# Gate and up projections by seven half-size products in a float32 encoder layer

## The chip, the core and the metric

The kernel runs on one core of a Trainium2 chip. The metric is the time of one execution on the device in microseconds; the number used is the median over runs. TensorE (PE in the profile) does matrix products, VectorE (DVE), ScalarE (ACT) and GpSimd (POOL) elementwise work, and SyncE (SP) issues the DMA transfers here. Products accumulate in PSUM banks of 128 partitions by 512 float32; everything else is staged in SBUF.

## The reference

One encoder layer and a last norm, for two sequences with the same weights: `x_prompt` of 512 tokens and `x_sample` of 1024, each of width 1024. Cut to what matters here:

```
x = x + hybrid_mixer(rmsnorm(x, norm1_g), w_in, ..., w_out)      # attention and linear attention
hn = rmsnorm(x, norm2_g)
x = x + (silu(hn @ w_gate) * (hn @ w_up)) @ w_down               # 1024 -> 2816 -> 1024
y = rmsnorm(x, final_norm_g)
```

All is float32. The 1536 tokens of both sequences go through the feed-forward part together, since it treats each token alone.

## The kernel before

A float32 product is made of three passes. Each operand is split into a high part `h` and a rest `l` (`split`, L66 to L69: the cast that makes `h` runs on ACT, L68, the subtraction that makes `l` on DVE, L69), and a product sums h·h, h·l and l·h in PSUM (`mm3`, L82 to L84, and in the same way L982).

The mixer comes first (up to L867): projections, attention, linear attention. Its end is the output projection of the second sequence (`Out`, tile `acco`, products at L82 to L84, added to the residual at L760). In between the last tiles of it the first six token tiles of the feed-forward part are made ready: `Block.rows` loads a tile of 128 tokens (`hx`, three buffers), squares and sums it on ACT (L898), scales it on DVE (L900); `Block.turn` transposes it on PE into a PSUM tile `trf` (L915) and splits that into `hbh` and `hbl`, the transposed input, 8 slices of the model dimension by 768 tokens.

The feed-forward part runs two blocks of 6 token tiles (768 tokens), and in each block 11 groups of 256 of the 2816 feed-forward columns:

- `raw_gu` (L924) loads the group's columns of `w_gate` and `w_up` (`rw_gate`, `rw_up`), `load_gu` splits them by tiles of 128 columns into `hw_gate` and `hw_up` (128 x 1024 elements each, L68 and L69).
- `gate_up` (L982): per tile of 128 columns, weight, slice of the model dimension and pass, two matmuls of 384 tokens into two banks `gu`; 8 slices x 3 passes x 2 halves of the tokens = 48 matmuls a tile and weight, 192 a group. ACT applies silu to gate (L989), DVE multiplies by up (L990) and the result is split into `g`.
- `down` of the group before stands behind the group's gate and up products: the weights `rd` (L999) are split into `wd`, 72 matmuls of 512 columns (L82 to L84) run into banks `dn`, and DVE adds each bank to the residual `xa` (L1018).
- At a block's last group `final` (L1035 to L1050) makes the last norm of each token tile and stores it.

Block 1's input is made ready while block 0 still has two `down` stages to run: the transposes stand between the steps of the last but one (L1059 to L1071), and the gate and up products of block 0's last group, which need the buffers `hbh` and `hbl`, are over by then.

What runs on an engine follows the order of its instruction stream, which a scheduler sets from the program's order; waits are on semaphores. Tiles come from pools with a fixed number of buffers, so a load into a tile waits until the last reader of the buffer that it takes has gone by: `wr` (raw weights) has three buffers, `wh` (split gate and up weights) four, `wd` three, `g` two, `hx` three.

## Time and profile before

| | us |
|---|---|
| median of three runs | 2030.09 (2027.62 to 2030.62) |
| span of the profiled execution | 2028.6 |
| PE busy | 2000.8 |
| DVE busy | 1042.3 |
| ACT busy | 715.2 |
| POOL busy | 80.9 |

The span is the time from the first to the last instruction of one execution under the profiler; it stands 1.5 us under the median of the runs. Busy time of an engine is the time in which an instruction of it was under way. PE's matmuls are pipelined: one that is listed with 0.34 us begins 0.17 us after the one before it, so the rate is read from the starts and not from the durations.

### The profile page before, as it was taken

Reading aid. Unit: us, or ns where it says so; the run is one execution under the profiler, and the core shown is the slowest. Engines: PE = TensorE matmul, PEld = TensorE weight load, DVE = VectorE, ACT = ScalarE, POOL = GpSimd, SP = SyncE. Lnnn points to the kernel's source line nnn. Section 1 sums busy time; section 2 is a strip of 40 time slices with the busy share of each in tenths; the row PEclk is TensorE's granted clock in tenths of the full one; section 3 lists DMA queues with packets and bytes.
Section 4 is the critical chain, followed back from the end, with each engine's and each line's share of the span. In section 5 each row is a group of like instructions: output and inputs, shape, how many; then the busy total and the mean of one; then the engine's idle time right before and its main releaser. Section 6 shows DMA issues by size and latency. Waiting matters only on the chain.

```text
span 2028.6 us, 31825 instructions
## 1 busy us (share of the span) xinstructions
PE 2000.8 (99%) x12740; PEld 1855.8 (91%) x12740; DVE 1042.3 (51%) x2500; ACT 715.2 (35%) x1730; POOL 80.9 (4%) x113
## 2 busy tenths in 40 slices
PE   8999999999999999999999999999999999999997
PEld 7888889899888889999999999999899999999996
DVE  5677766557576776444333333343633343333335
ACT  6665566455454554323111111211432211111112
POOL 1110010111000000000000000000110000000001
PEclk9999999999998999999999999999999999999999
DMA  5232221102220340855211111221341111211101
GB/s 144 61 100 73 65 80 35 51 26 68 68 79 17 105 137 29 284 175 187 63 63 63 63 63 63 63 63 63 114 167 63 63 63 63 63 63 63 63 22 63
DMA packets 149445, 163.13 MB, mean 80 GB/s; under 512 B 15856, under 2 KB 127536, under 8 KB 149296
## 3 DMA queue, kind: packets, MB, share of 16 engines
q1 hardware_dynamic: 149296, 161.09, 25.5%
q8 instruction: 100, 1.64, 0.3%
q14 instruction: 49, 0.40, 0.1%
HBM read 140.02 MB, written 21.04 MB: 79 GB/s over the span
## 4 chain that ended last, share of the span: by engine, by line
PE 92%; DMA 2%; DVE 2%; ACT 2%; issue 1%; POOL 1%; SPq 0%; POOLq 0%; DVEq 0%; ACTq 0%
PE gu L982 36%; PE acc L82 6%; PE acc L84 6%; PE acc L83 6%; PE dn L82 6%; PE dn L83 6%; PE dn L84 6%; PE sc L300 3%; PE pv L400 2%; PE acco L82 2%; PE trp L377 2%; PE acco L83 2%; PE acco L84 2%; PE kv L641 2%; PE trf L915 1%
## 5 line engine op out<-in xcount | busy, mean ns | idle before, releaser
L982 PE MATMUL gu<-hbh,hw_gate 128*128 128x384 f32 x1408 | 310.1, 336 | 0.0
L982 PE MATMUL gu<-hbh,hw_up 128*128 128x384 f32 x1408 | 308.5, 336 | 0.0
L982 PEld LDWEIGHTS gu<-hbh,hw_gate 128*128 128x128 f32 x1408 | 250.1, 188 | 1.8 <-ACT hbh L68 0.3
L982 PEld LDWEIGHTS gu<-hbh,hw_up 128*128 128x128 f32 x1408 | 249.9, 188 | 0.0
L1018 DVE TENSOR_TENSOR xa<-dn,xa 128x512 f32<-128x512 f32 x264 | 177.9, 689 | 113.7 <-PE dn L84 113.6
L83 PE MATMUL dn<-wd,g 128*128 128x512 f32 x528 | 205.5, 389 | 0.0
L84 PE MATMUL dn<-wd,g 128*128 128x512 f32 x528 | 205.4, 389 | 0.0
L82 PE MATMUL dn<-wd,g 128*128 128x512 f32 x528 | 205.3, 390 | 0.0
L982 PE MATMUL gu<-hbl,hw_gate 128*128 128x384 f32 x704 | 180.1, 336 | 0.0
L982 PE MATMUL gu<-hbl,hw_up 128*128 128x384 f32 x704 | 179.3, 336 | 0.0
L68 ACT CAST wd<-rd 128x1024 fp32r<-128x1024 f32 x44 | 45.9, 1049 | 378.0 <-PE dn L84 262.8
L990 DVE TENSOR_TENSOR e<-e,gu 128x384 f32<-128x384 f32 x88 | 44.8, 551 | 246.1 <-PE gu L982 246.1
L68 ACT CAST hw_up<-rw_up 128x1024 fp32r<-128x1024 f32 x44 | 46.2, 1049 | 278.4 <-PE gu L982 278.4
L69 DVE TENSOR_TENSOR hw_gate<-rw_gate,hw_gate 128x1024 fp32r<-128x1024 f32 x44 | 53.9, 1225 | 167.2 <-ACT hw_gate L68 167.2
L982 PEld LDWEIGHTS gu<-hbl,hw_gate 128*128 128x128 f32 x704 | 127.3, 188 | 0.0
L982 PEld LDWEIGHTS gu<-hbl,hw_up 128*128 128x128 f32 x704 | 127.2, 188 | 0.0
L84 PEld LDWEIGHTS dn<-wd,g 128*128 128x128 f32 x528 | 99.1, 188 | 20.7
L82 PEld LDWEIGHTS dn<-wd,g 128*128 128x128 f32 x528 | 99.1, 188 | 20.5 <-DVE xa L1018 0.7
L83 PEld LDWEIGHTS dn<-wd,g 128*128 128x128 f32 x528 | 99.2, 188 | 19.8 <-DVE wd L69 0.2
L69 DVE TENSOR_TENSOR wd<-rd,wd 128x1024 fp32r<-128x1024 f32 x44 | 54.1, 1236 | 108.7 <-ACT wd L68 108.7
L356 ACT ACTIVATE sm<-sm,st 128x256 f32<-128x256 f32 (+1 forms) x160 | 86.7, 543 | 58.4 <-DVE st L350 58.2
L989 ACT ACTIVATE e<-gu 128x384 f32<-128x384 f32 x88 | 38.5, 489 | 161.9 <-PE gu L982 161.9
(320 smaller groups left out, 4142.2 us busy)
## 6 DMA issues: line engine op xcount, KB each, us to landing
rw_gate<-w_gate SPq DMA_DIRECT2D x22, 1024.0 KB, 5.3
rw_up<-w_up SPq DMA_DIRECT2D x22, 1024.0 KB, 5.3
rd<-w_down SPq DMA_DIRECT2D x22, 1024.0 KB, 5.0
wr_ata<-w_in SPq DMA_DIRECT2D x32, 192.0 KB, 2.6
wr_atb<-w_in SPq DMA_DIRECT2D x32, 192.0 KB, 2.6
wt<-lsed SPq DMA_DIRECT2D x32, 128.0 KB, 3.2
mr_b<-mixd_b SPq DMA_DIRECT2D x8, 512.0 KB, 5.7
xr_b<-x_sample SPq DMA_DIRECT2D x8, 512.0 KB, 4.7
```

Source lines behind the costliest of these rows:

```text
L68: nc.scalar.copy(out=h, in_=src)
L69: nc.vector.tensor_tensor(out=l, in0=src, in1=h.bitcast(F32), op=ALU.subtract)
L82: nc.tensor.matmul(out, xh, wh, start=(k == 0), stop=False)
L83: nc.tensor.matmul(out, xh, wl, start=False, stop=False)
L84: nc.tensor.matmul(out, xl, wh, start=False, stop=(k == n - 1))
L300: nc.tensor.matmul(outs[hd], lhs(x[b:b + 64]), rhs(y[b:b + 64]), start=(n == 0), stop=(n == 2))
L356: nc.scalar.activation(out=sm[:, cs], in_=sm[:, cs], func=AF.Exp, scale=0.125, bias=st[:, NM, pat, hd, i0 + g:i0 + g + 1], accum_out=st[:, ...
L377: nc.tensor.transpose(tr[:, i], sm[:, i * P:(i + 1) * P], ident)
L400: nc.tensor.matmul(self.pv[b:b + 64, i * P:(i + 1) * P], v, ptt[hd][:, n], start=(first and n == 0), stop=(last and n == 3),)
L982: nc.tensor.matmul(ps[wi, hf], wt[:, part, k], src[:, k, hf * H:(hf + 1) * H], start=(k == 0 and part == 0 and src is hb), stop=(k == KD - ...
L990: nc.vector.tensor_tensor(out=e, in0=e, in1=ps[1, hf], op=ALU.mult)
L1018: nc.vector.tensor_tensor(out=acc[i][:, cs], in0=ps, in1=acc[i][:, cs], op=ALU.add)
```

## The change

Gate and up are no longer multiplied out directly. For a weight, a group and a block the product (256 columns of the weight, over 1024 of the model dimension, by 768 tokens) is cut into halves along all three: two tiles of 128 columns, two halves of the model dimension (KH = 4 slices each), and two halves of the tokens (even and odd token tiles, H = 384). The eight half-size products are replaced by seven of sums and differences of halves (the variant with shared partial sums):

- Inputs: seven matrices `b11, t2, b21, t3, t1, t4, b22`, each in a high and a low part, in place of `hbh` and `hbl`. `Block.turn(q)` makes them for a pair of token tiles: 16 transposes, one copy, four subtractions, seven splits. Three turns make a block, where there were six of two splits each.
- Weights: `Weights.prepare(n)` makes the operand of product n: `s1`, `s2` and two sums made in place in the raw tile (four DVE operations a weight, line L1004 of the new kernel) and seven splits of 128 x 512 (`cw_gate...`, `cw_up...`) in place of two splits of 128 x 1024.
- Products: `Group.product` runs 12 matmuls of 128 x 384 (4 slices x 3 passes) into one bank `gu`; products 2, 5 and 6 go on accumulating in the banks of 0, 3 and 4. Two weights x 7 x 12 = 168 matmuls a group in place of 192.
- Evictions: `common` copies product 0 (ACT, L1050 of the new kernel) and adds the others on DVE (L1047) into the partial sums `u2`, `u3` and `c21`, before silu and the multiplication, which are as many as before.
- Order of work: seven products of gate, `down` of the group before, seven products of up. Weights are prepared four products ahead (AHEAD). At the end of a block `down` of the last group stands directly behind its last up product, and the making of block 1's input stands between the steps of that last `down`.
- Buffers: `wr` 3 to 2 (and allocated only when the mixer's buffers are released), `wd` 3 to 2, `g` 2 to 1, `hx` 3 to 2, `wh` replaced by `wc` with six of half the size, `e` 3 to 7, new `sm` with two. The first group's raw weights are no longer loaded two tiles before the end of the output projection. `final` writes into `xa` in place, and its gain `fg` is loaded later.

```diff
         hb_p = pool(right, "hb", 1, side="right")
         cf = pool(right, "cf", 1, side="right")
-        hx_p = pool(right, "hx", 3, side="right")
+        hx_p = pool(right, "hx", 2, side="right")
         tf_p = pool(right, "tf", 3, side="right")
-        wr_p = pool(right, "wr", 3, side="right")
+        sm_p = pool(right, "sm", 2, side="right")
...
-        H = NT * P // 2
+        NP = NT // 2
+        H = NP * P
+        KH = KD // 2
...
-                self.hb = hb_p.tile([P, KD, NT * P], F32R, tag="h", name=f"hbh{blk}")
-                self.lb = hb_p.tile([P, KD, NT * P], F32R, tag="l", name=f"hbl{blk}")
+                self.B = {
+                    x: [hb_p.tile([P, KH, H], F32R, tag=f"{x}{w}", name=f"{x}{w}_{blk}") for w in "hl"]
+                    for x in ("b11", "t2", "b21", "t3", "t1", "t4", "b22")
+                }
                 self.acc, self.hx = {}, {}
...
+            def turn(self, q, tr_p, tag):
+                x = [self.hx.pop(2 * q), self.hx.pop(2 * q + 1)]
+                cs = slice(q * P, (q + 1) * P)
+                def quarter(k, t):
+                    tr = tr_p.tile([P, KH, P], F32, tag=tag, name="trf")
+                    for n in range(KH):
+                        nc.tensor.transpose(tr[:, n], x[t][:, (KH * k + n) * P:(KH * k + n + 1) * P], ident)
+                    return tr
+                def put(nm, src):
+                    h, l = self.B[nm]
+                    split(h[:, :, cs], l[:, :, cs], src)
+                sub = lambda o, i0, i1: nc.vector.tensor_tensor(out=o, in0=i0, in1=i1, op=ALU.subtract)
+                t3, t1 = [sm_p.tile([P, KH, P], F32, tag="sm", name=n) for n in ("xt3", "xt1")]
+                tr = quarter(0, 1)
+                nc.scalar.copy(out=t3, in_=tr)
+                tr = quarter(0, 0)
+                put("b11", tr)
+                sub(t1, t3, tr)
+                tr = quarter(1, 1)
+                put("t1", t1)
+                sub(t1, tr, t1)
+                put("t2", t1)
+                sub(t3, tr, t3)
+                put("b22", tr)
+                tr = quarter(1, 0)
+                put("t3", t3)
+                put("b21", tr)
+                sub(t1, tr, t1)
+                put("t4", t1)
...
-            if j + 2 == sb.T:
-                for wn in ("w_gate", "w_up"):
-                    raw_gu(0, 0, wn)
...
+                blocks[0].rows(1)
+            if 0 <= q < NP:
+                blocks[0].turn(q, tr_p, "tr")
+                if q + 1 < NP:
+                    blocks[0].rows(2 * q + 2)
+                    blocks[0].rows(2 * q + 3)
-        wh_p = pool(left, "wh", 4, side="left")
-        wd_p = pool(left, "wd", 3, side="left")
-        g_p = pool(left, "g", 2, side="left")
-        e_p = pool(left, "e", 3, side="left")
+        wr_p = pool(left, "wr", 2, side="left")
+        wc_p = pool(left, "wc", 6, side="left")
+        wd_p = pool(left, "wd", 2, side="left")
+        g_p = pool(left, "g", 1, side="left")
+        e_p = pool(left, "e", 7, side="left")
...
+        class Weights:
...
+            def prepare(self, n):
+                r = raws[self.key]
+                a11, a12, a21, a22 = [r[:, KH * k:KH * k + KH, P * f:P * f + P] for f in range(2) for k in range(2)]
+                tt = lambda o, i0, i1, op: nc.vector.tensor_tensor(out=o, in0=i0, in1=i1, op=op)
+                if n == 1:
+                    self.s1, self.s2 = [sm_p.tile([P, KH, P], F32, tag="sm", name=f"{x}{self.nm}") for x in ("s1", "s2")]
+                    tt(self.s1, a21, a22, ALU.add)
+                    tt(self.s2, self.s1, a11, ALU.subtract)
+                elif n == 3:
+                    tt(a21, a11, a21, ALU.subtract)
+                elif n == 6:
+                    tt(a12, a12, self.s2, ALU.subtract)
+                src = [a11, None, a12, a21, None, a22, a12][n]
+                src = self.s2 if n == 1 else self.s1 if n == 4 else src
+                wc = wc_p.tile([P, 2, KH, P], F32R, tag="wc", name=f"c{self.nm}{n}")
+                split(wc[:, 0], wc[:, 1], src)
+                self.w[n] = wc
+                if n == 6:
...
+            def product(self, wn, n):
+                x = ("b11", "t2", "b21", "t3", "t1", "t4", "b22")[n]
+                if n in (0, 1, 3, 4):
+                    self.ps = getattr(self, "ps", {})
+                    self.ps[n] = gu_p.tile([P, 512], F32, tag="gu", name="gu")[:, 0:H]
+                own = {2: 0, 5: 3, 6: 4}.get(n, n)
+                ps, wc, (xh, xl) = self.ps[own], self.w[wn].w.pop(n), self.b.B[x]
+                for k in range(KH):
+                    for i, (wp, src) in enumerate(((0, xh), (0, xl), (1, xh))):
+                        nc.tensor.matmul(ps, wc[:, wp, k], src[:, k], start=(own == n and k == 0 and i == 0),
+                                         stop=(k == KH - 1 and i == 2), skip_group_check=True)
+                getattr(self, wn)(n, ps)
+            def common(self, n, ps):
+                add = lambda o, i0: nc.vector.tensor_tensor(out=o, in0=ps, in1=i0, op=ALU.add)
+                if n == 0:
+                    self.u2 = self.tmp("u2")
+                    nc.scalar.copy(out=self.u2, in_=ps)
+                elif n == 1:
+                    add(self.u2, self.u2)
+                elif n == 3:
+                    self.u3 = self.tmp("u3")
+                    add(self.u3, self.u2)
+                elif n == 4:
+                    add(self.u3, self.u3)
+                    return (1, 1), self.u3
+                elif n == 5:
+                    c = self.tmp("c21")
+                    add(c, self.u2)
+                    return (1, 0), c
+                elif n == 6:
+                    add(self.u2, self.u2)
+                    return (0, 1), self.u2
+                return None, None
...
+            def w_up(self, n, ps):
+                if n == 0:
+                    self.gt = g_p.tile([P, 2, 2, 2, H], F32R, tag="g", name=f"g{self.blk}_{self.grp}")
+                if n == 2:
+                    at, c = (0, 0), ps
+                else:
+                    at, c = self.common(n, ps)
+                if at:
+                    f, t = at
+                    e = self.e.pop(at)
+                    nc.vector.tensor_tensor(out=e, in0=e, in1=c, op=ALU.mult)
+                    split(self.gt[:, f, 0, t], self.gt[:, f, 1, t], e)
...
+        AHEAD = 4
+        units = []
...
+            for grp in range(NG):
+                g = (blk, grp)
+                units += [("p", g, "w_gate", n) for n in range(7)]
+                if prev:
+                    units += [("d", prev, i) for i in range(NT)]
+                units += [("p", g, "w_up", n) for n in range(7)]
+                prev = g
+                if grp == NG - 1:
+                    units += [("d", prev, i) for i in range(NT)]
+                    prev = None
+        groups = {}
...
+        def prepare_to(m):
+            nonlocal ready
+            while ready < min(m, len(made)):
+                _, key, wn, n = made[ready]
+                if key[0] == 1 and len(blocks) < 2:
+                    blocks.append(Block(1))
+                fetch(key, wn)
+                group(key).w[wn].prepare(n)
+                if wn == "w_up" and n == 0:
+                    fetch(key, "w_down")
+                ready += 1
+        fg = ac_p.tile([P, D], F32, tag="fg", name="fg", bufs=1)
...
+        for u in units:
+            if u[0] == "p":
+                _, key, wn, n = u
+                last = key == (0, NG - 1)
+                ahead = AHEAD
+                prepare_to(done + ahead)
+                if key == (1, 0) and wn == "w_gate" and n == 0:
+                    blocks[1].residual()
+                group(key).product(wn, n)
+                done += 1
+                if wn == "w_up" and n in (3, 5):
+                    group(key).load_down((n - 3) // 2)
+                if last and wn == "w_up" and n in (2, 4):
+                    nb = blocks[1] if len(blocks) > 1 else Block(1)
+                    if len(blocks) < 2:
+                        blocks.append(nb)
+                    nb.rows((n - 2) // 2)
+            else:
+                _, key, i = u
+                group(key).down(i)
+                if key == (0, NG - 1) and i % 2 == 0:
+                    q = i // 2
+                    nb = blocks[1]
+                    nb.turn(q, dn_p, "dn")
+                    if q + 1 < NP:
+                        nb.rows(2 * q + 2)
+                        nb.rows(2 * q + 3)
```

DVE, from the last eviction of a `down` stage into the products behind it. Before: `xa` the residual, `wd` the split down weights, `hw_...` the split gate and up weights of the next group, `e` and `g` the activated product and its split.

```order
L1018 TENSOR_TENSOR xa05_11409<-dn_13000,xa05_11409 128x512 [waits PE_49]
L69 TENSOR_TENSOR wd041_13250<-rd04_13245,wd041_13250 128x1024 [waits Activation_49]
L69 TENSOR_TENSOR wd050_13588<-rd05_13586,wd050_13588 128x1024 [waits DMAHW5_49,Activation_49]
L69 TENSOR_TENSOR hw_gate012_13354<-rw_gate06_13349,hw_gate012_13354 128x1024 [waits DMAHW3_49,PE_49,Activation_49]
L990 TENSOR_TENSOR e_13119<-e_13119,gu_13069 128x384 [waits PE_49]
L990 TENSOR_TENSOR e_13124<-e_13124,gu_13070 128x384 [waits DVE_49,PE_49]
L69 TENSOR_TENSOR hw_up012_13357<-rw_up06_13351,hw_up012_13357 128x1024 [waits DMAHW4_49,Activation_49]
L69 TENSOR_TENSOR g0_5_13012<-e_13119,g0_5_13012 128x384 [waits Activation_49]
L69 TENSOR_TENSOR g0_5_13012<-e_13124,g0_5_13012 128x384 [waits Activation_49]
L69 TENSOR_TENSOR hw_gate013_13470<-rw_gate06_13349,hw_gate013_13470 128x1024 [waits PE_49,Activation_49]
```

The same place after: `u2`, `u3` the partial sums, `cw_...` the split operand of one product, `s1`, `s2` and `rw_gate06` the sums of weight quarters, `e11` the activated product.

```order
L69 TENSOR_TENSOR wd050_13553<-rd05_13327,wd050_13553 128x1024 [waits DMAHW2_49,Activation_49]
L69 TENSOR_TENSOR wd051_13602<-rd05_13327,wd051_13602 128x1024 [waits Activation_49]
L69 TENSOR_TENSOR cw_up056_13535<-rw_up05_13322,cw_up056_13535 128x512 [waits PE_49,Activation_49]
L1047 TENSOR_TENSOR u205_13497<-gu_13502,u205_13497 128x384 [waits PE_49]
L1088 TENSOR_TENSOR e1105_13301<-e1105_13301,gu_13483 128x384 [waits PE_49]
L69 TENSOR_TENSOR g0_5_13496<-e1105_13301,g0_5_13496 128x384 [waits Activation_49]
L1004 TENSOR_TENSOR s1w_gate06_13578<-rw_gate06_13556 128x512 [waits DMAHW3_49]
L1047 TENSOR_TENSOR u305_13551<-gu_13538,u205_13497 128x384 [waits PE_49]
L69 TENSOR_TENSOR cw_gate060_13558<-rw_gate06_13556,cw_gate060_13558 128x512 [waits Activation_49]
L1004 TENSOR_TENSOR s2w_gate06_13579<-s1w_gate06_13578,rw_gate06_13556 128x512 [waits DVE_49]
L1004 TENSOR_TENSOR rw_gate06_13556<-rw_gate06_13556 128x4x128
L1047 TENSOR_TENSOR u305_13551<-gu_13561,u305_13551 128x384 [waits DVE_49,PE_49]
```

Between a `down` stage and the next, DVE had ten splits and four multiplications spread over 192 matmuls; now the evictions of a product (L1047), which free its bank or feed its successor, stand in one stream with the weight sums of the next group, and the first of these, `s1w_gate06`, waits for a transfer.

DVE at the boundary of the blocks. Before: `hbl1` the split transposed input of block 1, `ms_n213` and `hx` the norm of one of its token tiles, `xa` evictions of block 0's last but one `down`.

```order
L1018 TENSOR_TENSOR xa01_11401<-dn_14996,xa01_11401 128x512 [waits PE_49]
L1018 TENSOR_TENSOR xa01_11401<-dn_15004,xa01_11401 128x512 [waits PE_49]
L69 TENSOR_TENSOR hbl1_14959<-trf_15012,hbh1_14958 128x4x128 [waits Activation_49]
L69 TENSOR_TENSOR hbl1_14959<-trf_15019,hbh1_14958 128x4x128 [waits Activation_49]
L1018 TENSOR_TENSOR xa02_11403<-dn_15036,xa02_11403 128x512 [waits PE_49]
L1018 TENSOR_TENSOR xa02_11403<-dn_15044,xa02_11403 128x512 [waits PE_49]
L69 TENSOR_TENSOR hbl1_14959<-trf_15052,hbh1_14958 128x4x128 [waits Activation_49]
L69 TENSOR_TENSOR hbl1_14959<-trf_15059,hbh1_14958 128x4x128 [waits Activation_49]
L1018 TENSOR_TENSOR xa03_11405<-dn_15076,xa03_11405 128x512 [waits PE_49]
L61 TENSOR_SCALAR ms_n213_15071<-ss_15068 128x1 [waits Activation_49]
L900 SCALAR_TENSOR_TENSOR hx_15066<-hx_15066,rs_n213_15073,g2_10608 128x1024 [waits DMAHW7_49,Pool_49]
```

The same place after, in block 0's last `down`: `b11l` to `t4l` the low parts of the seven inputs, `xt1` and `xt3` their differences, `ss` the sum of squares of the last norm.

```order
L69 TENSOR_TENSOR t1l_1_15413<-xt1_15545,t1h_1_15412 128x4x128 [waits Activation_49]
L930 TENSOR_TENSOR xt1_15545<-trf_15560,xt1_15545 128x512 [waits DVE_49]
L930 TENSOR_TENSOR xt3_15544<-trf_15560,xt3_15544 128x512
L1109 TENSOR_TENSOR xa02_11453<-dn_15635,xa02_11453 128x512 [waits PE_49]
L69 TENSOR_TENSOR t2l_1_15407<-xt1_15545,t2h_1_15406 128x4x128 [waits Activation_49]
L69 TENSOR_TENSOR b22l_1_15417<-trf_15560,b22h_1_15416 128x4x128 [waits Activation_49]
L69 TENSOR_TENSOR t3l_1_15411<-xt3_15544,t3h_1_15410 128x4x128 [waits DVE_49,Activation_49]
L930 TENSOR_TENSOR xt1_15545<-trf_15573,xt1_15545 128x512 [waits DVE_49]
L1109 TENSOR_TENSOR xa02_11453<-dn_15643,xa02_11453 128x512 [waits PE_49]
L61 TENSOR_SCALAR ms_n212_15590<-ss_15587 128x1 [waits Activation_49]
L1124 TENSOR_TENSOR ss_15651<-ss_15651 128x1
L906 SCALAR_TENSOR_TENSOR hx_15585<-hx_15585,rs_n212_15592,g2_10608 128x1024 [waits DMAHW4_49,Pool_49]
```

Two evictions used to have two splits between them; now a pair of `down` tiles has seven splits, four subtractions and the last norm of block 0 between its evictions, and the scaling of the next pair (`hx_15585`) stands behind most of that.

## Rows read from the trace of the kernel before

**Rows 1.** The page: span and busy time of the engines.

```profile
span 2028.6 us, 31825 instructions
...
PE 2000.8 (99%) x12740; PEld 1855.8 (91%) x12740; DVE 1042.3 (51%) x2500; ACT 715.2 (35%) x1730; POOL 80.9 (4%) x113
```

**Rows 2.** Windows: length, busy PE, PEld, DVE, ACT, POOL (instructions), clock, DMA.

```profile
1201.13:1234.41 33.28, 33.28 (x193) 33.28 (x192) 8.68 (x10) 7.00 (x11) 0.00 (x0) 1.00 0.20 64
1234.41:1250.73 16.32, 16.32 (x73) 13.52 (x73) 10.51 (x16) 2.34 (x4) 0.00 (x0) 1.00 0.20 64
1440.00:1490.00 50.00, 49.97 (x265) 44.21 (x264) 37.73 (x64) 26.48 (x55) 12.23 (x14) 1.00 0.55 189
```

**Rows 3.** Timeline, PE: first matmuls of a group and of its down.

```profile
1201.13 0.52 PE L982 MATMUL gu<-hbh,hw_gate 128*128 128x384 f32 x2
...
1234.41 0.39 PE L82 MATMUL dn<-wd,g 128*128 128x512 f32 x1
```

**Rows 4.** Waits of PE over the whole span, the longest first.

```profile
PE trn L162 <- DMA wr_vag<-w_in: 8.0, 1, 8.0
```

**Rows 5.** Timeline, PE: matmuls of one bank in the output projection.

```profile
899.33 0.33 PE L84 MATMUL acco<-wo,ml_b 128*128 128x384 f32 x1
899.50 0.33 PE L82 MATMUL acco<-wo,mh_b 128*128 128x384 f32 x1
```

**Rows 6.** DVE by line from 919 us: busy, mean ns, idle before.

```profile
L1018 DVE TENSOR_TENSOR xa<-dn,xa 128x512 f32<-128x512 f32 x264 | 177.9, 689 | 113.7 <-PE dn L84 113.6
L69 DVE TENSOR_TENSOR wd<-rd,wd 128x1024 fp32r<-128x1024 f32 x44 | 54.1, 1236 | 108.7 <-ACT wd L68 108.7
L69 DVE TENSOR_TENSOR g<-e,g 128x384 fp32r<-128x384 f32 x88 | 45.0, 552 | 0.2
L990 DVE TENSOR_TENSOR e<-e,gu 128x384 f32<-128x384 f32 x88 | 44.8, 551 | 246.1 <-PE gu L982 246.1
L69 DVE TENSOR_TENSOR hbl<-trf,hbh 128x512 fp32r<-128x512 f32 x14 | 8.9, 683 | 0.7 <-ACT hbh L68 0.7
```

**Rows 7.** Timeline, DVE: several of one kind, back to back.

```profile
1220.19 1.02 DVE L69 TENSOR_TENSOR g<-e,g 128x384 fp32r<-128x384 f32 x2
...
1436.23 1.88 DVE L1018 TENSOR_TENSOR xa<-dn,xa 128x512 f32<-128x512 f32 x3
```

**Rows 8.** ACT by line from 919 us, the same columns.

```profile
L68 ACT CAST g<-e 128x384 fp32r<-128x384 f32 x88 | 40.7, 508 | 16.1 <-DVE e L990 16.1
L68 ACT CAST hbh<-trf 128x512 fp32r<-128x512 f32 x14 | 7.6, 588 | 10.6 <-PE trf L915 10.4
L898 ACT ACTIVATE junk<-hx 128x1024 bf16<-128x1024 f32 x4 | 4.3, 1066 | 0.0
L898 ACT ACTIVATION_READ_ACCUMULATOR junk<-hx 128x1 f32 x4 | 0.8, 199 | 0.0
```

**Rows 9.** Timeline: load of a weight, and the cast that waits for it.

```profile
1203.18 0.37 SPq L999 DMA_DIRECT2D rd<-w_down  x1
1208.66 1.05 ACT L68 CAST wd<-rd 128x1024 fp32r<-128x1024 f32 x1 [6.96 <-DMA rd<-w_down]
```

**Rows 10.** One load with seven others behind it: issue, and time to landing.

```profile
L924 SPq DMA_DIRECT2D rw_up<-w_up x1: 383/383/383, 920.9 to 920.9; - x1
DMA to landing us min/median/max: 5.6/5.6/5.6
```

**Rows 11.** Tile hx: time to landing of its loads.

```profile
DMA to landing us min/median/max: 4.0/8.2/12.4
```

**Rows 12.** Timeline, DVE: a scaling of hx, behind the power on POOL.

```profile
1445.89 1.29 DVE L900 SCALAR_TENSOR_TENSOR hx<-hx,rs_n,g 128x1024 f32<-128x1024 f32 x1 [0.73 <-POOL rs_n L63]
```

**Rows 13.** Windows: the stretch of the attention with the lowest clock.

```profile
607.00:620.00 13.00, 13.00 (x52) 10.00 (x52) 7.73 (x33) 6.34 (x22) 0.00 (x0) 0.56 0.15 46
```

**Rows 14.** Timeline, PE: 384-column matmuls in that stretch.

```profile
611.56 0.52 PE L83 MATMUL acc<-w_atb,hnh_b 128*128 128x384 f32 x1
611.88 0.52 PE L84 MATMUL acc<-w_atb,hnl_b 128*128 128x384 f32 x1
```

174 lines of the change are left out of this document (68 added, 106 removed).

## Prediction

> **What bounds the kernel now.** I read the page first. PE is busy 2000.8 of 2028.6 us [rows 1], 98.6%, so the question is what PE does and whether it ever waits in the stage that is changed. The waits of PE answer the second: the longest in the whole run is 8.0 us for a weight of the mixer [rows 4], and from 919 us on, where the feed-forward part runs, PE has none in the list. Then the windows of one middle group, cut at the starts of its first gate matmul and of its first `down` matmul [rows 3]: 33.28 us for 192 gate and up matmuls and 16.32 us for 72 of `down`, PE busy throughout at full clock [rows 2], that is 2.4 GHz. So a 384-column matmul costs 33.28/192 = 0.1733 us and a 512-column one 16.32/72 = 0.227 us. DVE works 8.68 + 10.51 = 19.2 of these 49.6 us, ACT 9.3. At the boundary of the blocks PE is still busy 49.97 of 50 us, with DVE at 37.7 [rows 2]. The feed-forward part is bound by PE's stream alone, so fewer matmuls are worth their full price, if the others keep up.
>
> **What it removes.** 24 matmuls of 128x384 a group: 24 x 0.1733 = 4.16 us, 22 groups: **-91.5 us**. The number of matmuls is in the code and their form is unchanged. A product is now twelve matmuls in one bank in place of two banks taken in turn; the output projection runs such a stream already, and its starts lie 0.17 us apart [rows 5]. So the rate stays.
>
> **What the steady group must hide.** Ideal length now 168 x 0.1733 + 16.32 = 45.4 us. DVE goes from 26 to 54 operations. Priced by rows: 12 evictions of `down` at 0.69, 2 `wd` splits at 1.24, 8 multiplications and `g` splits at 0.55 [rows 6]; the 10 additions of partial sums read a bank as the multiplication does, 0.55; the 22 half-size weight sums and splits lie near half of `wd`'s (0.62) and the split of a 128x512 bank (0.68), I take 0.62. Sum 8.3 + 2.5 + 4.4 + 5.5 + 13.6 = 34 us. Back to back they start closer, 0.47 us for 384 columns (1.02 - 0.55) and 0.60 for 512 ((1.88 - 0.69)/2) [rows 7], which gives 31. That is 70 to 75% of 45.4 us: not the bound. ACT does 14 casts near 0.59, four at 0.51 [rows 8], four silus, two copies and two long casts, about 15 us: no bound either.
>
> Waits inside the group are the risk, as DVE now works in a stream of 54 with a load in it. I walked the order with these durations, T = 0 at the first up product; a product takes 12 x 0.1733 = 2.08 us. The raw weights have two buffers, so the next gate weight can only be loaded when the second `wd` split has read the down weight, T = 3.2. A load of that size took 5.5 us from issue to the cast that waited for it (1203.18 to 1208.66 [rows 9]), so it lands at 8.7. `s1w_gate06` waits for it on DVE, and behind it in the queue stands the first addition into `u3`, which must have read the bank of product 3 before product 5 goes on in it at 10.4: 8.7 + 0.7 + 0.5 = 9.9, half a microsecond early. The second `u3` addition stands behind three more half-size operations: 9.9 + 3 x 0.6 + 0.5 = 12.2, against product 6 at 12.5. So it fits by 0.3 us in the tightest place; gate's own products have 0.7 us and more. The six other weight operands are four products, 8 us, ahead of use. I put **+3 us** for 20 groups (0.15 each); bounds 0 and +20 (one microsecond a group, a load 1.3 us later).
>
> **Where the cover is gone.** (a) Start. The first gate weight used to be loaded two tiles ahead; its buffer now lies where the output projection's buffers were, and its load waits for PE to finish the middle chunk of the last tile. 24 matmuls of 256 columns are left then, by the two rates 0.12 us each, 2.9 us; the load takes 5.5, so 2.6 are uncovered; then a cast of 0.59 and a subtraction of 0.68 before the pass that needs the low part, and some 0.6 of hand-overs: **+4.5 us** (3 to 7). (b) In the output projection a pair of token tiles needs four subtractions and seven splits on DVE where it needed four splits, and both `hx` buffers must be emptied before the next pair loads. The chain from there to the next pair's second scaling is 8.7 to 12.9 us (worked out under (c)); a tile of the projection, 24 x (2 x 0.173 + 0.12) = 11.2 us, covers it to 1.7 us or wholly. With the longer queue on DVE I take 1.5 for each of two turns, **+3 us** (0 to 6).
>
> (c) The boundary of the blocks is the large one. Block 1's input used to be made behind two `down` stages; now it stands inside one, 72 matmuls and 48 transposes long, and the gate product behind it needs the result. Between two turns PE has two token tiles of `down`, 24 x 0.227 = 5.4 us. The next pair's loads wait for the last transpose of the turn before, then: landing 4.0 us at the shortest, 8.2 in the median [rows 11], two squares with their sums 2 x (1.07 + 0.20) [rows 8], the small operation and the power 0.15 + 0.73, the second scaling 1.29 [rows 12]. That is 8.7 to 12.9 us, if no queue holds it up, so PE idles 3.3 to 7.5 us in each of two turns; but on DVE the scaling stands behind splits and subtractions of the turn before, and on ACT the squares stand behind casts and the last norm. Walked along the queues I get 8.5 each. After the third turn `t2` and its like must be made while PE has one tile of `down` and one product: 2.5 us. After such pauses the clock can be at its lower level; a few microseconds of 24 matmuls at the lower rate cost some 2. Sum 17 + 2.5 + 2 = **+21.5 us**; bounds 6.6 (two times 3.3) and 32 (two times 12, 5 and 3).
>
> (d) The first group of each block has no `down` between gate and up, so its loads have 16 us less cover: **+1.5 us** (0 to 3). The last `down` ran alone at the end before and does after: **+0.3** (0 to 1). The transposes, the multiplications, silu and `down` are unchanged in number, and the DMA bytes too.
>
> Sum: -91.5 + 3 + 4.5 + 3 + 21.5 + 1.5 + 0.3 = -57.7. Against the profiled execution: 2028.6 - 57.7 = 1970.9; the median of the runs lies 1.5 us above that execution, so 1972.4, rounded to **1973**. All lower bounds together (-91.5 + 3 + 6.6 = -81.9) give 1948, all upper ones (-91.5 + 20 + 7 + 6 + 32 + 3 + 1 = -22.5) 2008. I choose mid values and not the low ends where the walk shows work in the same queue.
>
> **The clock.** The trace shows what it costs when it falls: in the attention stage, 607 to 620 us, after a stretch of short matmuls with gaps, the granted clock was 0.56 [rows 13], mostly the lower of its two levels (1.2 GHz), and 384-column matmuls started 0.32 us apart [rows 14] and not 0.173. In the feed-forward part it was 1.00 in each window, with a bank handed over every six matmuls of `down`. The Trainium skill, "TensorE: Matmul & The Clock Gate", section "A second HAM failure mode: psum-queue depth-cycling", speaks against this change: a kernel that goes round its PSUM banks idles a little between groups of matmuls, and that alone made its clock swing. `down` in this trace hands over banks without a swing, so the trace doesn't bear it out so far; but it has no accumulation that goes on in a bank which another engine has just read. What the rule would make of the time is worked out from rows as rival 2.
>
> **Rivals.**
> 1. *The load comes too late each time.* Gate's and up's raw weights are issued within a microsecond of each other; if they share the way and gate's lands when both are through, some 3.3 us later, `u3` comes 2.8 us late for product 5 in each of 20 groups: +56, the gain gone, 2029. For it: two buffers only. Against it: a load with seven others behind it still took 5.6 us [rows 10]. 5%.
> 2. *Slower: the clock falls in the products.* Place: products 5 and 6, which go on in a bank just read, 44 times each; if each hand-over leaves a gap, the products run at the lower level for a while. Price (0.32 - 0.173) x 168 = 24.7 us a group if all do, 543 in all; so it eats the 57 us from 10.6% of product time on, and at a quarter of it the time is 1972 + 136 = 2108. For it: the stretch of [rows 13, 14], and margins of 0.3 us. Against: a full clock in every window of the part. 6%.
> 3. *DVE becomes the bound.* 54 operations take the old 49.6 us if they cost 0.92 us each in the mean, waits for ACT's half of a split included, and hold PE from 0.84 on. The rows give 0.58 to 0.63, so half as much again would have to be lost in hand-overs: then 2025 to 2035. 4%.
> 4. *The boundary costs little* (its walk is the least sure): 1955. Inside the range of the forecast.
>
> **Chances.** Forecast, with its bounds and rival 4: 85%; rivals 1 to 3 15%, spread over no change and slower. A measurement of this kernel tells about 0.2%, 4 us, from no change. Of the 15%, milder forms worth 3 still end faster, 4 at no change, 8 slower: faster 0.88, same 0.04, slower 0.08. The likeliest case by itself is 1955 to 1995; the range for 8 in 10 takes in all the upper bounds together: 1950 to 2008.
>
> **What would show it.** Product starts 0.173 us apart and 45.4 to 45.7 us from group to group, and PE waits for `u3` near zero. A gap of 4 to 5 us before the first gate product. Two idle stretches of 8 us on PE between the transposes at the boundary, each ending with a scaling of `hx`. It is wrong if the groups are over 46.5 us long with PE waiting for DVE, or if the granted clock in the middle groups is under 0.98.

## The result and the profile after

The changed kernel takes 1971.41 us (median; 1969.79, 1971.00 and 1971.83 in the executions that are compared, against 2030.34 for the kernel before on the same chip). The ratio is 0.9706, with a 95% interval from 0.9691 to 0.9722. One more execution took 3734.6 us; it enters the median but no comparison.

The page after, span and busy time of the engines; it answers to [rows 1]:

```profile
span 1970.1 us, 31961 instructions
...
PE 1919.5 (97%) x12212; PEld 1769.0 (90%) x12212; DVE 1374.9 (70%) x3158; ACT 847.7 (43%) x2018; POOL 81.3 (4%) x113
```

PE has 528 matmuls less (12740 to 12212, which is 22 x 24) and 81 us less busy time; DVE has gained 333 us of work and PE is still the busy one. One group of the middle of block 0, from one first gate product to the next (columns as in [rows 2]):

```profile
1095.88:1141.33 45.45, 45.45 (x241) 42.63 (x241) 33.09 (x55) 14.83 (x26) 0.00 (x0) 1.00 0.21 70
```

It lasts 45.45 us, was 49.6, and PE is busy in all of it at the full clock, with DVE at 33.1 us (73%) and ACT at 14.8. PE's waits from the output projection on are few, and one place has nearly all of them:

```profile
PE trf L923 <- DVE hx L906: 16.1, 4, 8.4
PE gu L1042 <- ACT cw_gate L68: 3.5, 1, 3.5
PE dn L82 <- DVE xa L1109: 1.0, 1, 1.0
```

14.4 of the 16.1 us are two waits at the boundary of the blocks, 8.4 and 6.1; the rest are two small ones in the output projection. The 3.5 us are the start of the feed-forward part.

### The profile page after: what moved, and what is told of

It is laid out like the page before. It is cut to its first block, busy times and chain, and to the rows that moved or that the text cites. A ratio compares the mean times of both kernels' runs of the same rounds, so it can differ in the third digit from the quotient of the medians.

```text
span 1970.1 us, 31961 instructions
## 1 busy us (share of the span) xinstructions
PE 1919.5 (97%) x12212; PEld 1769.0 (90%) x12212; DVE 1374.9 (70%) x3158; ACT 847.7 (43%) x2018; POOL 81.3 (4%) x113
## 4 chain that ended last, share of the span: by engine, by line
PE 89%; DVE 4%; DMA 2%; ACT 2%; issue 1%; POOL 1%; SPq 0%; POOLq 0%; DVEq 0%; ACTq 0%
PE gu L1042 32%; PE acc L82 7%; PE acc L84 6%; PE acc L83 6%; PE dn L84 6%; PE dn L82 6%; PE dn L83 6%; PE sc L300 4%; PE pv L400 3%; PE trp L377 2%; PE acco L82 2%; PE acco L83 2%; PE acco L84 2%; PE kv L641 2%; DMA rw_gate<-w_gate 1%
## 5 line engine op out<-in xcount | busy, mean ns | idle before, releaser
L1047 DVE TENSOR_TENSOR u<-gu,u 128x384 f32<-128x384 f32 x176 | 97.3, 553 | 25.6 <-PE gu L1042 25.4
L68 ACT CAST cw_gate<-rw_gate 128x512 fp32r<-128x512 f32 x110 | 66.1, 620 | 110.4 <-DMA rw_gate<-w_gate 53.3
L82 PE MATMUL acc<-w_atb,hnh_b 128*128 128x384 f32 x256 | 91.7, 358 | 0.0
L68 ACT CAST cw_up<-rw_up 128x512 fp32r<-128x512 f32 x110 | 68.2, 621 | 51.2 <-PE gu L1042 49.5
L84 PE MATMUL acc<-w_atb,hnl_b 128*128 128x384 f32 x256 | 88.8, 347 | 0.0
L83 PE MATMUL acc<-w_atb,hnh_b 128*128 128x384 f32 x256 | 88.6, 346 | 0.0
L69 DVE TENSOR_TENSOR cw_up<-rw_up,cw_up 128x512 fp32r<-128x512 f32 x110 | 75.5, 688 | 7.9 <-ACT cw_up L68 7.2
L69 DVE TENSOR_TENSOR cw_gate<-rw_gate,cw_gate 128x512 fp32r<-128x512 f32 x110 | 75.2, 685 | 0.1
L377 PE MATMUL trp<-ident,sm 128*128 128x128 f32 x384 | 62.4, 288 | 0.8 <-ACT ptt L382 0.3
L82 PE MATMUL acco<-wo,mh_b 128*128 128x384 f32 (+1 forms) x192 | 61.5, 320 | 0.1
L83 PE MATMUL acco<-wo,mh_b 128*128 128x384 f32 (+1 forms) x192 | 61.2, 319 | 0.0
L84 PE MATMUL acco<-wo,ml_b 128*128 128x384 f32 (+1 forms) x192 | 61.2, 319 | 0.0
```

The costliest lines, as they stand in the source:

```text
L68: nc.scalar.copy(out=h, in_=src)
L69: nc.vector.tensor_tensor(out=l, in0=src, in1=h.bitcast(F32), op=ALU.subtract)
L82: nc.tensor.matmul(out, xh, wh, start=(k == 0), stop=False)
L83: nc.tensor.matmul(out, xh, wl, start=False, stop=False)
L84: nc.tensor.matmul(out, xl, wh, start=False, stop=(k == n - 1))
L377: nc.tensor.transpose(tr[:, i], sm[:, i * P:(i + 1) * P], ident)
```

## The experiments

Beside the median, two stretches are read from the timeline of each run: "boundary" is from the first matmul of block 0's last `down` to the first up product of block 1's second group. Without any wait it holds two `down` stages (2 x 16.33), three times seven products (3 x 14.56) and the 48 transposes (6.1, by which they lengthened the same work before), 82.4 us. "Feed-forward" is from the first gate product to the end of the span. Both leave out the mixer, whose code never changes but whose end (the start of the last product of the attention) lay between 819.5 and 824.9 us in these runs. The kernel before, taken beside each run, had medians from 2029.7 to 2031.6 us, so a difference of 2 us between two medians of this table says nothing by itself; the two stretches say more.

| run | median us | boundary | feed-forward |
|---|---|---|---|
| changed kernel | 1971.4 | 104.3 | 1042.3 |
| placement | 1966.5 | 104.5 | 1041.1 |
| squares in PSUM | 1973.5 | 108.2 | 1045.2 |
| late last norm | 1973.3 | 108.9 | 1045.7 |
| no norm | 1960.2 | 96.4 | 1031.9 |
| dummy transposes | 1968.5 | 104.5 | 1040.3 |
| early norm | 1960.5 | 95.6 | 1032.7 |
| early norm, placement, spread last norm | 1954.6 | 93.9 | 1029.9 |
| early norm, placement, GpSimd | 1955.3 | 94.6 | 1030.5 |
| all four | 1955.5 | 94.8 | 1030.3 |

**The number of matmuls by itself.** The kernel before, with one slice less in gate and up:

```diff
-                    for k in range(KD):
+                    for k in range(KD - 1):
```

> The kernel before with the last of the eight slices of the model dimension left out of the gate and up products (168 matmuls a group in place of 192, nothing else changed; the sums lack that slice). Theory PE-stream: only the number of matmuls counts, so 24 x 0.1733 x 22 = 91.5 us go, 2030.3 - 91.5 = 1938.8 us, groups of 45.4 us. Rival, the group has another bound or the short products a worse rate: groups over 45.7 us and a time over 1943 us.

1938.4 us (1935.9 and 1940.9). Its groups last 45.45 us, and a window inside one of them shows PE without a gap and DVE at its old 19.2 us of work:

```profile
1195.00:1240.00 45.00, 45.00 (x240) 42.18 (x239) 19.20 (x26) 9.36 (x14) 0.00 (x0) 1.00 0.22 71
```

So 24 matmuls a group are worth their 91.5 us, and 33 us is what the changed kernel loses on top of its products.

**The start.** The raw weights in another place:

```diff
-        wr_p = pool(left, "wr", 2, side="left")
         wc_p = pool(left, "wc", 6, side="left")
+        wr_p = pool(left, "wr", 2, side="left")
```

> The changed kernel with the pool of raw weights allocated behind that of the split operands, so that it lies over output weights that PE has read about 21 matmuls (3.6 us) earlier. Theory late-load: the first load is issued 3.6 us earlier, PE's gap of 3.5 us before the first gate product shrinks to under 0.5 us, the clock stays at its upper level, so the 2.4 us of slow matmuls behind the gap go too: 1971.4 - 5.5 = 1966 us. Rival, the gap is the chain cast and subtraction behind the load, or the load ends no sooner: gap over 2 us, 1970 to 1971 us.

1966.5 us, ratio to the kernel before 0.9674 (0.9654 to 0.9694). The first gate product now follows the output projection at once, but its third matmul waits (timeline, PE and DVE):

```profile
925.72 0.34 PE L1042 MATMUL gu<-b11h,cw_gate 128*128 128x384 f32 x1
925.90 0.33 PE L1042 MATMUL gu<-b11l,cw_gate 128*128 128x384 f32 x1
...
925.92 0.42 DVE L760 TENSOR_TENSOR xr_b<-acco,xr_b 128x256 f32<-128x256 f32 x1 [2.31 <-PE acco L84]
926.27 0.68 DVE L1004 TENSOR_TENSOR s1w_gate<-rw_gate 128x512 f32<-128x512 f32 x1
926.86 0.69 DVE L69 TENSOR_TENSOR cw_gate<-rw_gate,cw_gate 128x512 fp32r<-128x512 f32 x1
...
927.60 0.61 PE L1042 MATMUL gu<-b11h,cw_gate 128*128 128x384 f32 x2 [1.37 <-DVE cw_gate L69]
```

The load was the larger part of the pause, as the first theory says; the rest is the rival's: the low part stands on DVE behind the last residual sum (L760), which waits for PE itself, and behind `s1`. From the last attention product to the first gate product it gains 3.1 us (102.0 to 98.9) and in the first seven gate products 1.0 (17.2 to 16.2), 4.1 of the 5.5 expected; the remainder of the 5 us between the medians is within what the mixer varies.

**What holds PE at the boundary.** Three runs belong together here. In the changed kernel the second turn reads so (timeline; SP, DVE, ACT and PE in order of time):

```profile
1414.39 0.39 PE L82 MATMUL dn<-wd,g 128*128 128x512 f32 x1
...
1419.19 1.71 SPq L901 DMA_DIRECT2D hx<-x2d_b  x2
...
1428.05 0.68 DVE L69 TENSOR_TENSOR t3l<-xt,t3h 128x512 fp32r<-128x512 f32 x1
...
1428.76 1.06 ACT L904 ACTIVATE junk<-hx 128x1024 bf16<-128x1024 f32 x1 [0.67 <-DVE t3l L69]
...
1433.50 1.28 DVE L906 SCALAR_TENSOR_TENSOR hx<-hx,rs_n,g 128x1024 f32<-128x1024 f32 x1 [0.54 <-POOL rs_n L63]
...
1434.84 3.68 PE L923 MATMUL trf<-ident,hx 128*128 128x128 f32 x16 [8.35 <-DVE hx L906]
...
1458.02 0.34 PE L1042 MATMUL gu<-b11h,cw_gate 128*128 128x384 f32 x1
```

The load is issued at 1419.2, but the squares start at 1428.8, released by `t3l`: they write to one of two scratch tiles that `xt3` and `xt1` hold until then. That load and the next tile's had landed by 1424.7, four microseconds earlier. And DVE has little room all the while, as three windows show (DVE is the fourth figure):

```profile
1420.00:1430.00 10.00, 5.52 (x23) 3.75 (x21) 9.55 (x18) 6.79 (x17) 0.00 (x0) 1.00 0.31 105
1430.00:1440.00 10.00, 5.16 (x24) 4.87 (x25) 8.04 (x15) 5.81 (x11) 5.89 (x6) 0.66 0.22 88
1440.00:1450.00 10.00, 4.44 (x18) 2.83 (x16) 9.55 (x19) 7.13 (x17) 1.61 (x3) 0.93 0.62 226
```

Two theories: the scratch tile (or the whole chain from it), and DVE's full queue. First the scratch was taken away; the squares go to PSUM:

```diff
-                junk = sm_p.tile([P, D], BF16, tag="sm", name="junk")
+                    for c in range(2):
+                        junk = gu_p.tile([P, 512], F32, tag="gu", name="junk")
```

> The changed kernel with the squares of block 1's tokens written to a PSUM bank (two halves of 512) and not to the two scratch tiles that the differences xt1 and xt3 use. Theory scratch: the squares waited for the scratch tile of xt3 (they start at 1428.76, behind its last reader t3l), not for their load; freed of it they start some 3 us earlier, PE's two waits for hx (8.4 and 6.1 us) shrink by 2 to 3 us each, 1971.4 - 5 = 1966.5 us. Rival DVE-full: DVE is busy 87% of the 40 us there and the scaling stands in its queue, so PE's waits change by less than 1 us each and the time stays at 1970 to 1972 us.

1973.5 us. PE's waits for `hx` at the boundary are 15.0 us, not less, and the boundary is 3.9 us longer:

```profile
1424.78 0.60 ACT L907 ACTIVATE junk<-hx 128x512 f32<-128x512 f32 x1 [3.39 <-DMA hx<-x2d_b]
...
1434.26 0.15 DVE L61 TENSOR_SCALAR ms_n<-ss 128x1 f32<-128x1 f32 x1
...
1435.13 1.28 DVE L913 SCALAR_TENSOR_TENSOR hx<-hx,rs_n,g 128x1024 f32<-128x1024 f32 x1 [0.60 <-POOL rs_n L63]
```

The squares did start 4 us earlier, released by their load, and all was lost again on DVE: the second tile's small operation stands there until 1434.3, 6.4 us after its squares, behind the splits, subtractions and evictions that precede it in the queue. (The edit also put an addition for each tile into that queue; at the first DVE stood idle for 1.5 us.) Scratch alone is not the cause. Then DVE was lightened: block 0's last norms moved behind the first gate products of block 1.

```diff
+                    if not end and self.blk == 0:
+                        late.append(lambda: final(0, acc, i, si, j))
+                        return
...
+                if late:
+                    late.pop(0)()
```

> The changed kernel with the last norm of block 0's six token tiles moved behind the first six gate products of block 1. 12 evictions stay at the boundary; 5 scalings of 0.75 us and 12 small operations leave DVE there (5.5 us), 12 squares and 5 multiplications leave ACT (13 us). Theory DVE-full: with that much less in the queues the scalings of hx come sooner, PE's waits for hx (14.4 us) fall by 4 to 6 us, 1966 us. Rival scratch/load: the squares wait for the scratch tile or the load all the same, waits fall by under 2 us, 1970 us.

1973.3 us, waits of 14.5 us at the boundary. The squares wait for `t3l` as before, as the rival says, and DVE has its gap only behind the scalings:

```profile
1424.94 0.68 DVE L69 TENSOR_TENSOR t3l<-xt,t3h 128x512 fp32r<-128x512 f32 x1
...
1425.65 1.06 ACT L904 ACTIVATE junk<-hx 128x1024 bf16<-128x1024 f32 x1 [1.29 <-DVE t3l L69]
...
1430.40 1.28 DVE L906 SCALAR_TENSOR_TENSOR hx<-hx,rs_n,g 128x1024 f32<-128x1024 f32 x1 [0.73 <-POOL rs_n L63]
...
1434.36 0.69 DVE L69 TENSOR_TENSOR b11l<-trf,b11h 128x512 fp32r<-128x512 f32 x1 [2.68 <-ACT b11h L68]
```

What was moved came back in block 1's first group, which got 4.9 us longer. The run does not test a full queue, though. Up to `t3l` DVE is as busy as before (no gap over 0.5 us from 1414.5 to 1425.6), since the work that was moved stood almost wholly behind the scalings; and from the end of `t3l` to the end of the second scaling it takes 6.1 us in both kernels. So block 0's last norm is not what the scaling waits for. What is left is an order: DVE works through the turn, `t3l` at the end of that releases the scratch tile, and squares, power and scaling follow in series; with the scratch freed the second scaling stands behind the same turn in DVE's queue. Whether a shorter queue before `t3l` and a free scratch tile together would end the pause was not run. That left the whole chain to be removed:

```diff
+                if self.blk:
+                    self.hx[i] = hx
+                    return
```

> The changed kernel without the norm of block 1's input (no squares, no scaling; its tiles are turned as loaded). Theory chain: the pause is load, squares, power, scaling and what stands before the scaling in DVE's queue; with the load alone (5.0 us) against two token tiles of down (5.4 us) PE's waits fall from 14.4 us to under 2 us, and the low clock after them goes too: 1971.4 - 17 = 1954 us. Rival DVE-full: only the six scalings (7.7 us of DVE) count, waits of 6 us or more stay, 1964 us.

1960.2 us: no wait for `hx` is left at the boundary, and it is 7.9 us shorter, not 17. DVE is now full in most of it:

```profile
1430.00:1440.00 10.00, 8.62 (x43) 6.29 (x42) 9.86 (x18) 7.58 (x17) 2.66 (x3) 0.99 0.39 147
1440.00:1450.00 10.00, 6.53 (x26) 5.71 (x27) 9.85 (x20) 5.59 (x12) 2.09 (x3) 0.86 0.59 211
```

Both expectations were half right: the waits for `hx` go as the chain theory says, but 8.4 us of shorter waits for other tiles stand in their place (the longest 2.3 us), as the other says, and the gain at the boundary is near the 7.7 us of DVE work that it counted. Another 2.2 us of this run's gain lie in the first seven products, where the clock did not fall this time.

**All of the boundary's work left out.** Block 1 uses block 0's input:

```diff
-                    nb.turn(q, dn_p, "dn")
+                    pass
```

> The changed kernel without the making of block 1's input (no loads, norms, transposes, differences or splits of it; block 1 uses block 0's input). Theory: all of the boundary's loss hangs on it, 21.3 us of pauses and low clock and 48 transposes x 0.115 = 5.5 us: 1971.4 - 26.8 = 1944.6 us, and down of the last group runs 16.3 us. Rival, block 0's last norm beside it is what holds PE: 5 us or more of waits stay, 1949 us and over.

1945.8 us (1943.6 and 1948.0), feed-forward 1016.4, 25.9 less than the changed kernel, near the 26.8 of the first theory. The two `down` stages and three times seven products of the boundary take 78.4 us, 2.1 over their 76.3 without waits: block 0's last norm by itself holds PE by no more than that.

**Room in the steady group.** The low part of each split weight operand made twice:

```diff
                 split(wc[:, 0], wc[:, 1], src)
+                tt(wc[:, 1], src, wc[:, 0].bitcast(F32), ALU.subtract)
```

> The changed kernel with the low part of every split gate and up operand made twice: 14 more DVE operations of 0.6 us a group, DVE 41.5 of 45.45 us busy. Theory narrow margins: the additions into u3 have 0.2 to 0.4 us to spare before products 5 and 6, so groups get longer by 0.3 to 0.9 us, 1978 to 1990 us, with PE waits for u3. Rival, only the sum of DVE's work counts while it is under the group's length: 1971 to 1973 us.

1980.3 us (1978.8 and 1981.7). Eight groups in the middle of block 0 last 45.52 to 46.07 us, 0.1 to 0.6 longer, with DVE at 40.2 of 45 us:

```profile
1095.00:1140.00 45.00, 45.00 (x239) 42.02 (x238) 40.18 (x67) 14.78 (x26) 0.00 (x0) 1.00 0.22 71
```

The margins are narrow and the loss is real, mostly at or under the low end of what was expected for each group; 3.0 of the 10.8 us in the feed-forward part fell at block 0's last `down` and 1.0 in the first group. The list of waits has a single one in these eight groups (0.15 us); the starts of the products show the rest. In each gate stage the first addition into `u3` ends 0.15 us before product 5, which starts up to 0.5 us late; in this one, which began at 1369.17, it came 10.67 us after the start and not 10.40:

```profile
1379.15 0.55 DVE L1048 TENSOR_TENSOR u<-gu,u 128x384 f32<-128x384 f32 x1
...
1379.84 0.41 PE L1043 MATMUL gu<-t4h,cw_gate 128*128 128x384 f32 x1
```

**The clock.** Transposes of the identity in the pauses:

```diff
+                    nc.tensor.transpose(tr[:, k % 4], ident, ident)
...
+        warm(25)
...
+                    warm((0, 50, 36)[q])
```

> The changed kernel with transposes of the identity that nobody reads: 25 before the first gate product, 50 and 36 before the second and third turn of the boundary, to fill PE's pauses there. Theory clock: the pauses stay and the work behind them runs at the upper level, 2.4 us less in the first group, 3.4 us less in the 32 transposes after the two long waits, 5 to 6 us in all, 1966 us. Rival, DVE and ACT set the pace behind the pauses: 2.4 us less, 1969 us.

1968.5 us (1964.7 to 1973.8), which is not clear of the changed kernel: the ratio is 0.970 with an interval from 0.968 to 0.972. At the boundary the 16 transposes of the second turn ran in 1.97 us where they had taken 3.68; the dummies of the third came too early to help:

```profile
1427.04 1.97 PE L923 MATMUL trf<-ident,hx 128*128 128x128 f32 x16 [1.54 <-DVE hx L906]
...
1442.74 3.67 PE L923 MATMUL trf<-ident,hx 128*128 128x128 f32 x16 [6.29 <-DVE hx L906]
```

The boundary stayed at 104.5 us. So the low clock behind the first pause costs nothing, since ACT and DVE set the pace there, as the rival says; behind the second pause it was not put to the test. The first seven products took 15.0 us in place of 17.2. How much of that is the dummies' doing can't be said: they took 15.0 in the run without norm too, with the pause and without dummies, and 16.6 in the run with the late last norm.

**Versions that gain.** The norm of block 1's tokens is made early, one tile in each of six groups of block 0, stored, and only loaded at the boundary:

```diff
+                nc.vector.scalar_tensor_tensor(out=hx, in0=hx, scalar=rs, in1=g2, op0=ALU.mult, op1=ALU.mult)
+                nc.sync.dma_start(out=hnd[i * P:(i + 1) * P, :], in_=hx)
...
+                    nc.sync.dma_start(out=self.hx[i], in_=hnd[i * P:(i + 1) * P, :])
...
+                if i == 2 and key[0] == 0 and 2 <= key[1] < 8:
+                    Block.early(key[1] - 2)
```

> The changed kernel with the norm of block 1's input made early: in six groups of block 0 one token tile each is loaded, normed and stored, and the boundary only loads the normed tiles. Theory two limits: at the boundary the chain squares, power, scaling binds first and DVE's full queue second; with the chain gone the boundary and the first gate products get 8 us shorter, as without any norm, and the six groups pay under 0.3 us each: 1971.4 - 7 = 1964 us. Rival chain alone: PE's pauses all go, 14 us or more, 1957 us. Rival narrow margins: the scaling of 1.3 us in the six groups holds PE by 1 us and more each, 1970 us.

1960.5 us, ratio 0.9653 (0.9639 to 0.9668), midway between the first theory's 1964 and the second's 1957. The boundary is 8.8 us shorter, about as with no norm at all and near the 8 of the first theory, and the six groups keep their 45.45 us, so the third theory fails. DVE is as full as there:

```profile
1434.00:1444.00 10.00, 8.28 (x41) 6.23 (x41) 9.86 (x18) 7.51 (x17) 2.60 (x3) 1.00 0.37 136
```

Two ways to take work off DVE were added to that and to the placement. First block 0's last norms, one behind every second product of block 1's first group:

```diff
+                if late and key[0] == 1 and n % 2:
+                    late.pop(0)()
```

> The early norm, the other placement of the raw weights, and block 0's last norms spread behind every second product of block 1's first group. Theory two limits: DVE's queue is what is left at the boundary, so 5.5 us of scalings and small operations less there make it 5 us shorter on top of the 8 (early norm) and 3 (placement): 1971.4 - 16 = 1955 us. Rival, the cost moves into the next group as in the late norm by itself (3.6 us): 1960 us.

1954.6 us, ratio 0.9619 (0.9604 to 0.9635), the lowest median, though its interval overlaps those of the two runs that follow. The time is the one that the theory gave, but not by its steps: the boundary gains 1.6 us over the early norm, not 5, since block 1's first up products take 17.8 us in place of 14.6; most of it moved, as the rival says. Then, in place of the spread, two of the seven low parts on GpSimd:

```diff
+                    if self.blk and nm in ("t3", "t4"):
+                        nc.scalar.copy(out=h[:, :, cs], in_=src)
+                        nc.gpsimd.tensor_tensor(out=l[:, :, cs], in0=src, in1=h[:, :, cs].bitcast(F32), op=ALU.subtract)
+                        return
```

> The early norm and the other placement, and at the boundary the low parts of t3 and t4 made on GpSimd and not on DVE (six of 0.6 us; nobody waits for them before the fourth and sixth gate product, but the scratch tiles come free later). Theory two limits: 3.6 us of DVE less make the boundary 3 us shorter: 1971.4 - 8 - 3 - 3 = 1957 us. Rival, GpSimd needs 1.3 us for each and holds the scratch tiles that the next turn needs: no gain over the other two, 1960 us and over.

1955.3 us, ratio 0.9630 (0.9614 to 0.9646), boundary 1.0 us under the early norm's; a third of what was expected. While GpSimd works, some of DVE's own operations get slower (last section). And all together:

> All together: early norm, other placement, block 0's last norms spread over block 1's first group, low parts of t3 and t4 at the boundary on GpSimd. Theory two limits: DVE's queue is what is left, the two ways to shorten it add up: from the start of block 0's last down to block 1's first down 3 us less than in either alone (77.6 and 78.3 us), 75 us, and 1952 us in all. Rival, something else is next (transposes waiting for evictions of their banks, the first gate products for the casts): 77 us or more, 1954 us.

1955.5 us, ratio 0.9630 (0.9616 to 0.9644): the gains don't add up, the boundary is 94.8 us. DVE is no longer full there; its windows from 1410 to 1470 us have 8.1 to 9.4 of 10 us, as this one:

```profile
1430.00:1440.00 10.00, 9.62 (x51) 7.57 (x50) 9.30 (x17) 5.37 (x11) 2.58 (x2) 1.00 0.00 0
```

What binds the last 12 us of the boundary is not settled; no single wait of PE there is over 1.7 us. By place, 5.7 of them lie in block 1's first group from its up products on (18.3 and 16.5 us for seven products, in place of 14.6 each), where the spread norms stand.

## Why the prediction was right

1973 us were predicted (1972.4 by the sum) and 1971.4 measured. By its own terms, from the two profiled executions:

| term | predicted | measured |
|---|---|---|
| 528 matmuls | -91.5 | -91.5 (group 45.45, with the one-slice-less kernel as a check) |
| steady groups | +3 | +0.8: three of the groups are 0.2 to 0.4 us longer, the others not |
| (a) start | +4.5 | +3.6, and 2.7 of slow products behind it |
| (b) output projection | +3 | +3.4 |
| (c) boundary | +21.5 | +21.2 (43.6 - 16.3 - 6.1) |
| (d) first groups | +1.5 | +0.7 (the second block's; the first's is under the start) |
| last down | +0.3 | -0.3 |
| mixer, unchanged | 0 | +1.3, which is within its variation |

The sum, -58.1, gives 1970.5 against a span of 1970.1. The gain and the places of the loss were right. That the total is right to 2 us is in part luck: the start cost 1.8 us more than was put down for it and the steady groups 2.2 us less.

*The steady group.* The walk along DVE's queue was good to 0.3 us. Timeline of one group, up products, T = 0 at 1217.85:

```profile
1221.04 0.37 SPq L991 DMA_DIRECT2D rw_gate<-w_gate  x1
...
1226.84 0.69 DVE L1004 TENSOR_TENSOR s1w_gate<-rw_gate 128x512 f32<-128x512 f32 x1 [0.85 <-DMA rw_gate<-w_gate]
1227.44 0.55 DVE L1047 TENSOR_TENSOR u<-gu,u 128x384 f32<-128x384 f32 x1
...
1228.25 0.34 PE L1042 MATMUL gu<-t4h,cw_up 128*128 128x384 f32 x1
...
1229.71 0.55 DVE L1047 TENSOR_TENSOR u<-gu,u 128x384 f32<-128x384 f32 x1
...
1230.41 0.42 PE L1042 MATMUL gu<-b22h,cw_up 128*128 128x384 f32 x1
```

The load came at 9.0 (8.7 predicted), the two additions into `u3` ended at 10.1 and 12.4 (9.9 and 12.2), and products 5 and 6 began at 10.4 and 12.6. This is one of the three longer groups: product 6 was due at 12.5 and waited, and the 0.15 us between the end of the addition and its start are the hand-over (0.15 in each of the three). In an ordinary group (T = 0 at 1126.77) the second addition ends at 12.1 and product 6 starts on time:

```profile
1138.33 0.55 DVE L1047 TENSOR_TENSOR u<-gu,u 128x384 f32<-128x384 f32 x1
...
1139.25 0.34 PE L1042 MATMUL gu<-b22h,cw_up 128*128 128x384 f32 x1
```

There 0.37 us lie between them, so 0.2 us beyond a hand-over are to spare. That is why the 3 us were not needed, and why 14 more DVE operations hurt at once. Rival 1, the late load, did not come about.

*The clock.* Rival 2 did not occur: the granted clock is 1.00 in the groups, though products 5 and 6 go on in banks that DVE or ACT has just read. The rule of the Trainium skill ("TensorE: Matmul & The Clock Gate", section "A second HAM failure mode: psum-queue depth-cycling") speaks of a PE that idles a little between groups of matmuls while it goes round its banks. This stream goes round them without a gap between the products, so it does not put the rule to the test. The clock fell elsewhere, behind the pause at the start and in the boundary, and there the prediction had it the wrong way round: 2 us at the boundary, where the dummy transposes show that behind the first pause it costs nothing, and none at the start, where the granted clock is 0.50 for 5.3 us behind the pause:

```profile
924.00:927.70 3.70, 0.27 (x3) 0.06 (x1) 1.12 (x2) 0.62 (x1) 0.00 (x0) 0.83 1.09 365
927.70:933.00 5.30, 5.28 (x16) 5.06 (x17) 4.99 (x8) 3.18 (x6) 0.00 (x0) 0.50 1.04 399
```

*The boundary.* Size and place were right, the mechanism only in part, and that 21.5 met 21.2 is luck: the pauses were 2.6 us smaller than predicted and the rest 2.3 us larger. Predicted were two pauses of 8.5 us, each ending with a scaling of `hx`; measured 8.4 and 6.1. Of the other 6.8 us, where 4.5 were predicted, 3.3 are what the 32 transposes behind the pauses took longer at the lower clock and 1.5 are short waits; the dummies show that at least behind the first pause DVE and ACT would have taken that time anyway. The prediction had the chain start at the load and be held up in the queues. The load set nothing (it had landed four microseconds before the squares began): the squares waited for a scratch tile, which the prediction did not see, and that tile came free at the end of DVE's work on the turn, the queue which it did see. Freeing the scratch tile alone left the pause (15.0 us), since the scaling stands behind the same work; that the queue and the scratch tile are each enough without the other is not shown.

*Rival 3* (DVE the bound) is wrong for the steady group, 73%. At the boundary DVE is full once the chain is gone (9.6 to 9.9 us of 10), but taking work off it there gave only 1.0 and 1.6 us, so it is not the only limit.

## What to carry to other kernels

Where one engine is busy throughout, work taken off it is worth its measured rate; the loss is to be sought where the new stream has no cover (its start, and where one block's end makes the next one's input), and there it is found by walking the queues in their order with measured durations. If a pause stays after its releaser has been taken away, look at what stands before the waiting operation in its own engine's queue; and before work is moved off an engine to end a pause, see that it stands ahead of the operation that is waited for, and not behind it. And work with its own inputs ready early (here a norm) belongs in the stage that has room, not at the seam.

## What was not expected of the hardware

- The clock after a pause is not the same each time. Behind 3.5 us without a matmul it was 0.50 for 5.3 us; in the run without norm, behind a pause of 3.1 us at the same place, the window over the pause and the products behind it shows 1.00 (in five other runs, behind pauses of 3.1 to 3.2 us there, windows of 5 to 6 us show 0.50 to 0.72):

```profile
925.00:930.00 5.00, 3.65 (x19) 3.33 (x20) 4.39 (x7) 3.07 (x6) 0.00 (x0) 1.00 1.03 366
```

- GpSimd's work and DVE's can slow each other. GpSimd took 1.27 to 1.30 us for five of its six subtractions of 128x512, which take DVE 0.68, and 1.75 for the sixth, which ran beside DVE's scalings of `xa`; three such scalings took 4.52 us there, up to 1.79 each, where one takes 0.75 with GpSimd idle (in the changed kernel two such scalings beside GpSimd's work kept their 0.75 and one took 1.76). So moving `t3l` and `t4l` may have cost DVE part of what it saved; how much was not separated:

```profile
L948 POOL TENSOR_TENSOR t4l<-xt,t4h 128x512 fp32r<-128x512 f32 x3 | 4.3, 1445 | 2.6 <-ACT t4h L947 2.6
...
1445.55 4.52 DVE L1156 SCALAR_TENSOR_TENSOR xa<-xa,rs_nf,fg 128x512 f32<-128x512 f32 x3
...
1447.78 1.75 POOL L948 TENSOR_TENSOR t4l<-xt,t4h 128x512 fp32r<-128x512 f32 x1
```

Not every DVE operation suffers: `b21l<-trf,b21h`, which reads a PSUM tile, took 0.69 us beside GpSimd's work in the same run, and `t1l<-xt,t1h`, which reads none, 1.43:

```profile
1428.08 0.69 DVE L69 TENSOR_TENSOR b21l<-trf,b21h 128x512 fp32r<-128x512 f32 x1
...
1429.28 1.43 DVE L69 TENSOR_TENSOR t1l<-xt,t1h 128x512 fp32r<-128x512 f32 x1
```
